# A table of offsets on the priorities of a list schedule

## The chip, the core and the metric

The kernel runs on one core of a Trainium2 chip. The core has engines that run side by side, each with its own queue of instructions: TensorE (PE in the profile, its weight loads PEld), VectorE (DVE), ScalarE (ACT), GpSimd (POOL), and SyncE (SP), which here only issues DMAs. The metric is the device time of one execution in microseconds; of several runs the median counts. TensorE's clock has two levels, 2.4 and 1.2 GHz; the profile's granted clock is 1.00 when a whole stretch was at the higher one.

## What is computed

The reference runs two networks one after the other on x (512 tokens, width 1024), in float32:

```python
# first_block
for i in range(2):
    h = rmsnorm(x, norm_mix[i])
    y = conformer_conv_module(h, ...) if i == 0 else nsa_attention(h, ...)
    x = x + y
    x = x + swiglu_ffn(rmsnorm(x, norm_ffn[i]), ...)
# second_block
for layer in range(2):
    mix = mamba2_mixer(h, ...) if layer == 0 else stick_breaking_attention(h, ...)
    h = layer_norm(ALPHA * h + mix, ...)
    h = layer_norm(ALPHA * h + squared_relu_mlp(h, ...), ...)
```

So there are eight phases, named conv, ffn0, nsa, ffn1, mamba, mlp0, sb and mlp1 in the kernel. The attention of nsa has 16 heads in 4 groups, rotary positions on a part of each head, compressed blocks and causal softmax.

## The kernel before

x lies in SBUF as eight tiles x_1 to x_8 of 128 features by 512 tokens, and every phase works on all 512 tokens. Each float32 product is made of three matmuls with operands split in a high and a low part (mm3: xh with whi at L135, xl with whi at L136, xh with wlo at L137); a product of one 128-column block of a weight with all of x is 8 x 3 = 24 matmuls of 128x512. Weights come by DMA from SyncE (wraw, L106), ACT rounds the high part (whi, L95) and DVE or POOL subtracts (wlo, L96), or, in other phases, ACT and an adding DMA make wlo (L121 to L123). Activations are split in the same way (L95/L96, L210/L211).

In the phase conv the queue of SyncE brings the first weight of the input projection, the tap weights of the depthwise convolution (conv_taps; their split parts are wh and wl) and the tiles of x.

In nsa each group of heads has a projection of k and four heads' worth of q. The rotation, turn (L773), copies parts of the rows by four small DMAs into sw, multiplies sw by the sines (L781, POOL) and x by the cosines (L782, POOL) and adds both (L783, DVE). For k the result tk is then spread by DMA and split (kdh, kdl); for q it is split into qa and qb (L1535 to L1538). scores (L986) makes the score block of a head in three PSUM banks (L997 to L1002), takes the negative maximum of each of its four parts (nmx, L1005, DVE), then the exponentials (pr, L1008, ACT); the banks are free after these. The probabilities are scaled (L1014, L1016), transposed (L1027), split (pth, ptl) and multiplied with v (L1041). compress makes a product with 160 columns for the compressed blocks, and L1057 the scores against these.

Layer norms of the second network are computed for two halves of the tokens (class HalfNorm; L312 and L314 add up sums, L329 adds squares, L162 and L152 to L156 make the scale rr by a Newton iteration, L183 turns it by TensorE), the second half beside the first matmuls of what follows.

What sets the order: the kernel's functions record all instructions of the program, each with a priority (the place in the program less an offset by a name, PRIO, given by pri). Then class Arrange (L1741) takes all instructions of the program, builds their dependences, prices each one, and runs a list schedule over all engines: schedule keeps one list of instructions for each engine, sorted by priority, and takes from it the first that could start at once, else the one that could start first; for SyncE it is always the first whose buffer is free. It models buffers, the DMA queue, the port shared by DVE and POOL, ACT's function tables and TensorE's two speeds. Its result, the order of each engine's instructions and of the takers of each buffer, is what apply (L1993) fixes. On the chip each engine runs its instructions in that order, and each waits for what it depends on.

Of the kernel before, what the change touches and what calls it, by code (L numbers as in the profile page):

```python
# [2134 lines left out]
```

## Time and profile before

| | |
|---|---|
| runs | 2943.2, 2943.57, 2951.58 us; median 2943.57 |
| profiled execution | 2945.75 us, of which span 2944.0 us, mean granted clock 0.97 |
| busy: TensorE, VectorE, ScalarE, GpSimd | 2792.5, 1710.5, 1488.9, 457.3 us |
| conv, ffn0 | to 250, to 600 us |
| nsa, ffn1 | 600 to 1050, to 1390 us |
| mamba, mlp0 | 1390 to 1900, to 2250 us |
| sb, mlp1 | 2250 to 2600, to 2944 us |

The times of the phases are rounded from the timeline. TensorE is the engine that is busy nearly all the time; how it stands in a stretch is read from the windows (busy time against length, and the granted clock), and what it waited for from the waits, where "A <- B" means that A was released by B. In timelines the bracket at the end of a row is the idle time of the engine ahead of it and what ended it.

### The profile page before, as it was taken

The page shows a single profiled execution, that of the slowest core. Times are in us where ns is not written, and L with a number is a line of the kernel's source. Part 1 is how long each engine was busy: PE and PEld are TensorE (multiplying, and loading weights), DVE is VectorE, ACT ScalarE, POOL GpSimd, SP SyncE. Part 2 cuts the span into 40 slices and gives each one's busy share as a digit, 9 for nine tenths or more (in the row PEclk, how much of TensorE's full clock was granted, in tenths as well). Part 3 has the DMA queues.
Part 4 walks back from the last instruction along what each step waited for, and adds up shares of the span by engine and source line. Part 5 has one row for each costly group of instructions (what it writes and reads, how often), then busy time and mean ns, then how long its engine had stood idle before and what let it go on. Part 6 is the DMA issues. An engine that isn't in the chain of part 4 may idle for free.

```text
span 2944.0 us, 38136 instructions
## 1 busy us (share of the span) xinstructions
PE 2792.5 (95%) x14613; PEld 2388.8 (81%) x14613; DVE 1710.5 (58%) x2946; ACT 1488.9 (51%) x2319; POOL 457.3 (16%) x440
## 2 busy tenths in 40 slices
PE   8989999999898899999999999799999999799997
PEld 7878888878777788887787878788888888788887
DVE  8976344546877944444775756743326566743335
ACT  4354222336566632223886877443334888543333
POOL 0010000034222100001111212400015222500004
PEclk9989999998999999999999999799999999899998
DMA  5323323221111133333556565333333544433232
GB/s 190 122 82 123 100 90 103 88 71 53 47 43 48 44 94 94 94 102 104 129 135 151 132 156 126 111 108 98 96 95 113 122 115 94 136 94 98 95 95 92
DMA packets 94919, 300.33 MB, mean 102 GB/s; under 512 B 11280, under 2 KB 13840, under 8 KB 94736
## 3 DMA queue, kind: packets, MB, share of 16 engines
q1 hardware_dynamic: 80192, 253.71, 27.6%
q0 software_dynamic: 14544, 44.18, 7.9%
q8 instruction: 115, 1.88, 0.3%
q14 instruction: 68, 0.56, 0.1%
HBM read 246.33 MB, written 2.10 MB: 84 GB/s over the span
## 4 chain that ended last, share of the span: by engine, by line
PE 57%; ACT 4%; DVE 3%; DMA 2%; issue 2%; POOL 0%; SPq 0%; ACTq 0%; POOLq 0%; DVEq 0%
PE mm L137 17%; PE mm L135 17%; PE mm L136 17%; DMA wlo<-wraw 2%; PE z L1670 1%; PE mm L1686 1%; DVE s L329 1%; PE e L1434 0%; ACT th L95 0%; ACT whi L121 0%; DVE x L538 0%; PE mm L1041 0%; PE st L183 0%; ACT s L1436 0%; ACT wlo L122 0%
## 5 line engine op out<-in xcount | busy, mean ns | idle before, releaser
L95 ACT ACTIVATE whi<-wraw 128x1024 fp32r<-128x1024 f32 (+2 forms) x383 | 385.1, 1009 | 1000.1 <-PE mm L136 769.0
L135 PE MATMUL mm<-xh,whi 128*128 128x512 f32 (+1 forms) x2240 | 849.2, 383 | 25.1 <-ACT whi L95 12.5
L137 PE MATMUL mm<-xh,wlo 128*128 128x512 f32 (+1 forms) x2240 | 851.2, 382 | 5.0 <-DMA wlo<-wraw 3.0
L136 PE MATMUL mm<-xl,whi 128*128 128x512 f32 (+1 forms) x2240 | 850.1, 381 | 0.9 <-DVE xl L543 0.6
L135 PEld LDWEIGHTS mm<-xh,whi 128*128 128x128 f32 x2240 | 425.9, 192 | 106.7 <-ACT whi L95 15.3
L137 PEld LDWEIGHTS mm<-xh,wlo 128*128 128x128 f32 x2240 | 427.5, 191 | 88.0 <-DMA wlo<-wraw 5.9
L136 PEld LDWEIGHTS mm<-xl,whi 128*128 128x128 f32 x2240 | 427.5, 191 | 78.2 <-DVE xl L543 1.7
L135 PE MATMUL mm<-hh,whi 128*128 128x512 f32 (+1 forms) x1344 | 483.3, 361 | 5.9 <-ACT whi L95 3.2
L137 PE MATMUL mm<-hh,wlo 128*128 128x512 f32 (+1 forms) x1344 | 483.2, 360 | 5.7 <-DMA wlo<-wraw 4.7
L136 PE MATMUL mm<-hl,whi 128*128 128x512 f32 (+1 forms) x1344 | 482.7, 360 | 0.9 <-DVE hl L96 0.9
L96 POOL TENSOR_TENSOR wlo<-wraw,whi 128x1024 fp32r<-128x1024 f32 (+2 forms) x119 | 255.1, 2155 | 1364.2 <-ACT whi L95 1342.5
L96 DVE TENSOR_TENSOR wlo<-wraw,whi 128x1024 fp32r<-128x1024 f32 (+1 forms) x264 | 316.3, 1200 | 183.6 <-ACT whi L95 180.8
L137 PEld LDWEIGHTS mm<-hh,wlo 128*128 128x128 f32 x1344 | 256.0, 191 | 44.1 <-DMA wlo<-wraw 6.0
L135 PEld LDWEIGHTS mm<-hh,whi 128*128 128x128 f32 x1344 | 256.0, 191 | 43.7 <-ACT hh L95 3.8
L136 PEld LDWEIGHTS mm<-hl,whi 128*128 128x128 f32 x1344 | 256.0, 191 | 36.9 <-DVE hl L96 1.4
L287 DVE TENSOR_TENSOR x<-x,mm 128x512 f32<-128x512 f32 x80 | 55.0, 687 | 222.3 <-PE mm L137 222.3
L123 POOL DMA_DIRECT2D wlo<-wraw x101 | 87.6, 867 | 485.8 <-ACT wlo L122 344.2
L96 DVE TENSOR_TENSOR hl<-s,hh 128x512 fp32r<-128x512 f32 (+1 forms) x120 | 88.2, 736 | 77.2 <-ACT hh L95 77.1
L121 ACT ACTIVATE whi<-wraw 128x1024 fp32r<-128x1024 f32 (+2 forms) x101 | 92.1, 912 | 75.8 <-PE mm L136 57.9
L503 DVE TENSOR_TENSOR s<-mm,rstd 128x512 f32<-128x512 f32 x44 | 30.4, 691 | 136.0 <-PE mm L137 136.0
L95 ACT ACTIVATE hh<-s 128x512 fp32r<-128x512 f32 (+1 forms) x120 | 75.7, 632 | 41.5 <-DVE s L504 27.3
L122 ACT ACTIVATE wlo<-wraw 128x1024 fp32r<-128x1024 f32 (+2 forms) x101 | 91.6, 908 | 8.0 <-PE mm L136 7.6
(459 smaller groups left out, 4072.1 us busy)
## 6 DMA issues: line engine op xcount, KB each, us to landing
wraw<-mlp_w SPq DMA_DIRECT2D x144, 512.0 KB
wraw<-ffn_w_in SPq DMA_DIRECT2D x88, 512.0 KB
wlo<-wraw POOLq DMA_DIRECT2D x68, 512.0 KB, 4.8
wraw<-ssm_w_in SPq DMA_DIRECT2D x48, 512.0 KB
wraw<-ffn_w_out SPq DMA_DIRECT2D x32, 448.0 KB
wraw<-conv_taps SPq DMA_DIRECT2D x20, 512.0 KB
wraw<-ssm_w_out SPq DMA_DIRECT2D x40, 256.0 KB
wraw<-conv_w_out SPq DMA_DIRECT2D x16, 512.0 KB
```

Of the source, the lines that this page charges most:

```text
L95: nc.scalar.activation(hi, x, AF.Copy)
L96: (eng or nc.vector).tensor_tensor(lo, x, hi.bitcast(F32), op=OP.subtract)
L121: self.nc.scalar.activation(hi[:, :n], raw[:, :n], AF.Copy)
L122: self.nc.scalar.activation(lo[:, :n], raw[:, :n], AF.Copy, scale=-1.0)
L123: self.nc.gpsimd.dma_start(lo[:, :n], raw[:, :n], accum_op=OP.add)
L135: mm(ps, ah, bh, start=start, stop=False)
L136: mm(ps, ah, bl, start=False, stop=False)
L137: mm(ps, al, bh, start=False, stop=stop)
L287: nc.vector.tensor_tensor(c.x[m], c.x[m], ps, op=OP.add)
L329: nc.vector.tensor_tensor(acc[m % 2], acc[m % 2], q, op=OP.add)
L503: nc.vector.tensor_tensor(u, pu, r, op=OP.mult)
L1670: nc.tensor.matmul(reg, w, part[:, ZOFF[jj]:ZOFF[jj] + S - jj * P], start=False, stop=True, skip_group_check=True)
```

## The change

A table DUE holds, for the phases conv, nsa, mamba and sb, an offset for each of 166 groups of instructions, from -2020 to +2520. A group is the engine, the name of the tile written and of the first two tiles read, without numbers ("DVE mx_nsp s_scr"; "D" for a tensor in DRAM). marks remembers where each phase begins in the list of instructions, and Arrange adds the group's offset of the phase to the priority of each instruction; a lower number is taken earlier. Nothing else is changed: the same instructions with the same operands and buffer sizes are scheduled, in another order. The closing norm of a phase, and the first weights of the phase behind it, belong to the phase. The search over the schedule's own estimate that the numbers are from is no part of the kernel.

```diff
@@ class Ctx @@
-        self.edges = []
+        self.edges, self.marks = [], []
...
+DUE = {
+    "conv": {
+        "DVE s_scr s_scr s_scr": -20, "DVE x2_xres x2_xres mm_pmm": -520, "DVE x4_xres x4_xres mm_pmm": -160, "DVE xl6_acts x6_xres par_const": 160,
...
+    "nsa": {
+        "ACT acc_acts hr_nq": -175, "ACT hh1_hid os_nsp": 80, "ACT pr_ntp mm_ps nmx_nsp": -705, "ACT pr_ntp pr_ntp sums_nsp": 5, "ACT pth_npp mm_ps": 5,
...
-    def __init__(self, tc, edges=()):
+    def __init__(self, tc, edges=(), marks=()):
...
         self.cost = [self.price(j) for j in range(n)]
+        self.due = [i.bass_priority or 0 for i in self.ins]
+        for (p, lo), hi in zip(marks, [m for _, m in marks[1:]] + [n]):
+            for j in range(lo, hi):
+                self.due[j] += DUE.get(p, {}).get(self.group(j), 0)
...
+    def group(self, j):
+        name = lambda a: self.tile(a).tag.rstrip("_0123456789") if self.tile(a) is not None else "D"
+        ins, outs = [[name(a) for a in x if hasattr(a, "ap")] for x in (self.ins[j].ins, self.ins[j].outs)]
+        return " ".join([("PE", "ACT", "DVE", "POOL", "SP", "", "")[self.eng[j]], (outs or ["-"])[0]] + ins[:2])
...
-        order, takers = self.schedule([i.bass_priority or 0 for i in self.ins])
+        order, takers = self.schedule(self.due)
...
             c.ph = p
+            c.marks.append((p, sum(len(b.instructions) for b in tc.nc.cur_f.blocks if b.name == tc.start_bb_name)))
...
-    Arrange(tc, c.edges).apply()
+    Arrange(tc, c.edges, c.marks).apply()
```

The order of SyncE's queue at the start. Rows are line, operation, tile written <- tensor read. Before:

```order
L106 DMA wraw_320<-conv_w_in 128x1024
L106 DMA wraw_403<-conv_taps 128x1024
L106 DMA wraw_409<-conv_taps 128x1024
L237 DMA par<-par 128x8
L242 DMA x_1_85<-x 128x512
L246 DMA wraw_93<-conv_w_in 128x512
L246 DMA wraw_94<-conv_w_in 128x512
L242 DMA x_2_86<-x 128x512
L242 DMA x_3_87<-x 128x512
L242 DMA x_4_88<-x 128x512
L246 DMA wraw_93<-conv_w_in 128x512
```

and now:

```order
L106 DMA wraw_320<-conv_w_in 128x1024
L237 DMA par<-par 128x8
L242 DMA x_1_85<-x 128x512
L246 DMA wraw_93<-conv_w_in 128x512
L246 DMA wraw_94<-conv_w_in 128x512
L242 DMA x_2_86<-x 128x512
L242 DMA x_3_87<-x 128x512
L242 DMA x_4_88<-x 128x512
L246 DMA wraw_93<-conv_w_in 128x512
L246 DMA wraw_94<-conv_w_in 128x512
L242 DMA x_5_89<-x 128x512
```

The two taps wraw_403 and wraw_409 go from ahead of x_1 to behind x_8 (six rows below the last one shown).

ACT in nsa, around the exponentials of one head (pr_7053; the tiles mm_7056, mm_7058 and mm_7057 are its scores, kdh the split of the next k, whi of later weights). Before:

```order
L1008 ACTIVATE pr_7053,sums_7055<-mm_7056,nmx_7054 128x128
L1008 ACTIVATE pr_7053,sums_7055<-mm_7056,nmx_7054 128x384
L95 ACTIVATE whi_7266<-wraw_7264 128x1024
L95 ACTIVATE whi_7533<-wraw_7531 128x1024
L95 ACTIVATE kdh_1242_7006<-s_7003 128x512
L95 ACTIVATE kdh_1245_7013<-s_7010 128x512
L1008 ACTIVATE pr_7053,sums_7055<-mm_7058,nmx_7054 128x512
L1008 ACTIVATE pr_7053,sums_7055<-mm_7057,nmx_7054 128x256
```

and now:

```order
L1008 ACTIVATE pr_7053,sums_7055<-mm_7056,nmx_7054 128x128
L1008 ACTIVATE pr_7053,sums_7055<-mm_7056,nmx_7054 128x384
L1008 ACTIVATE pr_7053,sums_7055<-mm_7058,nmx_7054 128x512
L1008 ACTIVATE pr_7053,sums_7055<-mm_7057,nmx_7054 128x256
L95 ACTIVATE hh_1247_7017<-os_6713 128x512
L95 ACTIVATE whi_7266<-wraw_7264 128x1024
L95 ACTIVATE pth_7154<-mm_7149 128x512
L1014 ACTIVATE pr_7053<-pr_7053,sums_7055 128x384
L95 ACTIVATE kdh_1242_7006<-s_7003 128x512
```

The four exponentials now stand in a row, ahead of the splits; a second head further on (pr_8010) has the same two orders.

DVE at the same place, the maxima of that head (nmx_7054) and the rotation of k (tk, L783). Before:

```order
L1016 TENSOR_SCALAR pr_6955<-pr_6955,sums_6957 128x128
L1016 TENSOR_SCALAR pr_6955<-pr_6955,sums_6957 128x256
L783 TENSOR_TENSOR tk_6605<-s_6993,s_6999 128x512
L96 TENSOR_TENSOR ptl_7050<-mm_7046,pth_7049 128x256
L96 TENSOR_TENSOR hl_1249_7019<-os_6713,hh_1247_7017 128x512
L1005 TENSOR_REDUCE nmx_7054<-mm_7058 128x1
L1005 TENSOR_REDUCE nmx_7054<-mm_7057 128x1
```

and now:

```order
L96 TENSOR_TENSOR ptl_7043<-mm_7037,pth_7042 128x512
L1005 TENSOR_REDUCE nmx_7054<-mm_7056 128x1 x2
L96 TENSOR_TENSOR ptl_7050<-mm_7046,pth_7049 128x256
L1005 TENSOR_REDUCE nmx_7054<-mm_7058 128x1
L1005 TENSOR_REDUCE nmx_7054<-mm_7057 128x1
L783 TENSOR_TENSOR tk_6605<-s_6993,s_6999 128x512
```

The rotation's sum went from ahead of the last two maxima to behind them.

POOL, two turns in nsa (s_6180 and s_6186, then s_6211 and s_6217). Before:

```order
L781 TENSOR_TENSOR s_6186<-sw_2483,sin_2446 128x512
L782 TENSOR_TENSOR s_6180<-s_6180,cos_2447 128x512
L96 TENSOR_TENSOR wlo_6577<-wraw_6574,whi_6576 128x1024
L1076 MEMSET pcz_6314 128x4x64
L781 TENSOR_TENSOR s_6217<-sw_2483,sin_2446 128x512
L782 TENSOR_TENSOR s_6211<-s_6211,cos_2447 128x512
```

and now:

```order
L782 TENSOR_TENSOR s_6180<-s_6180,cos_2447 128x512
L781 TENSOR_TENSOR s_6186<-sw_2483,sin_2446 128x512
L1076 MEMSET pcz_6314 128x4x64
L782 TENSOR_TENSOR s_6211<-s_6211,cos_2447 128x512
L781 TENSOR_TENSOR s_6217<-sw_2483,sin_2446 128x512
```

The product with the cosines (L782) comes ahead of that with sw (L781), here and in all 17 turns.

On TensorE the rows are the same with others between them: eight projections of 24 matmuls that stood in one piece in nsa stand in pieces of about 8 with scores, transposes and values between them, and the compress product stands among the pieces of a projection.

## Rows read from the trace of the kernel before

**Rows 1.** The page: busy time of each engine, and the chain that ended last.

```profile
PE 2792.5 (95%) x14613; PEld 2388.8 (81%) x14613; DVE 1710.5 (58%) x2946; ACT 1488.9 (51%) x2319; POOL 457.3 (16%) x440
...
PE 57%; ACT 4%; DVE 3%; DMA 2%; issue 2%; POOL 0%; SPq 0%; ACTq 0%; POOLq 0%; DVEq 0%
```

**Rows 2.** Windows: us, engines' busy time (count), granted clock, DMA share, GB/s.

```profile
250.00:600.00 350.00, 349.04 (x1525) 285.99 (x1524) 159.33 (x194) 102.69 (x128) 4.01 (x6) 1.00 0.29 92
...
sum 450.00, PE 403.46 PEld 344.16 DVE 328.59 ACT 260.98 POOL 121.53; mean PE 44.83 PEld 38.24 DVE 36.51 ACT 29.00 POOL 13.50
...
705.00:726.00 21.00, 17.40 (x90) 17.07 (x90) 8.26 (x27) 8.98 (x19) 7.30 (x4) 0.59 0.20 61
...
924.00:943.00 19.00, 14.99 (x65) 12.15 (x66) 13.37 (x36) 11.22 (x28) 2.62 (x2) 0.82 0.15 52
...
6.00:10.00 4.00, 0.00 (x0) 0.00 (x0) 3.31 (x4) 3.31 (x5) 0.00 (x0) 1.00 1.03 383
```

**Rows 3.** TensorE's waits, 600 to 1050: total us, times, longest.

```profile
PE mm L997 <- DVE qa L1537: 8.3, 2, 8.1
...
PE mm L997 <- ACT pr L1008: 5.7, 3, 2.7
...
PE mm L135 <- ACT v L95: 3.6, 1, 3.6
...
PE mm L1027 <- DVE tk L771: 2.9, 2, 1.6
...
PE mm L1041 <- DVE ptl L96: 2.8, 3, 1.2
```

**Rows 4.** Timeline from 0 to 14: start us, us, engine, line, operation.

```profile
7.75 1.06 ACT L95 ACTIVATE wh<-wraw 128x1024 fp32r<-128x1024 f32 x1 [0.28 <-DMA wraw<-conv_taps]
...
8.71 0.71 ACT L210 ACTIVATE xh<-x,par 128x512 fp32r<-128x512 f32 x1
...
10.51 0.80 PE L135 MATMUL mm<-xh,whi 128*128 128x512 f32 x1 [10.51 <-ACT whi L95]
```

**Rows 5.** Timeline from 820 to 847: rows of PE, DVE and ACT.

```profile
824.42 0.23 PE L1002 MATMUL mm<-cmask,identr 128*128 128x128 f32 x1
...
836.72 0.45 PE L997 MATMUL mm<-kdh,qb 128*128 128x128 f32 x1 [2.61 <-ACT pr L1008]
...
828.22 2.87 DVE L783 TENSOR_TENSOR tk<-s,s 128x512 f32<-128x512 f32 x1 [2.46 <-POOL s L782]
...
831.94 1.01 DVE L1005 TENSOR_REDUCE nmx<-mm 128x1 f32<-128x512 f32 x2
...
841.25 0.69 DVE L783 TENSOR_TENSOR t<-s,s 128x512 f32<-128x512 f32 x1 [1.17 <-POOL s L782]
...
834.14 0.63 ACT L95 ACTIVATE kdh<-s 128x512 fp32r<-128x512 f32 x1 [1.97 <-DMA s<-tk]
...
835.91 0.67 ACT L1008 ACTIVATE pr<-mm,nmx 128x512 f32<-128x512 f32 x1
```

**Rows 6.** Timeline from 752 to 768: rows of POOL, DVE and PE.

```profile
759.37 1.28 POOL L781 TENSOR_TENSOR s<-sw,sin 128x512 f32<-128x512 f32 x1 [1.36 <-DMA sw<-s]
...
760.59 1.28 POOL L782 TENSOR_TENSOR s<-s,cos 128x512 f32<-128x512 f32 x1
...
762.08 2.82 DVE L783 TENSOR_TENSOR t<-s,s 128x512 f32<-128x512 f32 x1
...
766.44 0.48 PE L997 MATMUL mm<-kdh,qa 128*128 128x128 f32 x1 [8.05 <-DVE qa L1537]
```

**Rows 7.** TensorE's waits, 1390 to 1900.

```profile
PE mm L137 <- DMA wlo<-wraw: 7.7, 9, 2.2
```

**Rows 8.** Timeline from 1873 to 1892: rows of DVE and POOL.

```profile
1877.86 5.45 DVE L329 TENSOR_TENSOR s<-s,s 128x256 f32<-128x256 f32 x3 [3.46 <-ACT s L328]
...
1873.28 12.23 POOL L96 TENSOR_TENSOR wlo<-wraw,whi 128x1024 fp32r<-128x1024 f32 x5 [0.49 <-ACT whi L95]
```

**Rows 9.** TensorE's waits, 2250 to 2600.

```profile
PE st L183 <- DVE rr L156: 8.5, 2, 4.5
```

More of the change, by code (lines that the diff above doesn't have):

```diff
@@ L1738, in sb_phase @@
         closing(c, "sb_w_o", [a[4:] + b for a, b in zip(hs, late[0])], 1, "lnmix1", head)
+DUE = {
+    "conv": {
+        "ACT hh7_hid y7_convy": 120, "ACT s_scr y1_convy": 585, "DVE hl5_hid y5_convy hh5_hid": -80, "DVE rsq_small rsq_small rv_small": 410,
+        "DVE s_scr s_scr s_scr": -20, "DVE x2_xres x2_xres mm_pmm": -520, "DVE x4_xres x4_xres mm_pmm": -160, "DVE xl6_acts x6_xres par_const": 160,
+        "DVE y3_convy st_pst y3_convy": 960, "DVE y3_convy y3_convy st_pst": 320, "PE mm_pmm hh5_hid whi_wts": 20, "PE mm_pmm hh5_hid wlo_wts": 630,
+        "PE mm_pmm hl1_hid whi_wts": 640, "PE mm_pmm hl7_hid whi_wts": 290, "PE mm_pmm ul_convu wh_convt": 110, "PE mm_pmm xh1_acts whi_wts": 310,
+        "PE st_pst ones_const acc_acts": -640, "SP wraw_convr D": 160, "SP x5_xres D": 20, "SP x6_xres D": 140, "SP x7_xres D": -950
+    },
+    "nsa": {
+        "ACT acc_acts hr_nq": -175, "ACT hh1_hid os_nsp": 80, "ACT pr_ntp mm_ps nmx_nsp": -705, "ACT pr_ntp pr_ntp sums_nsp": 5, "ACT pth_npp mm_ps": 5,
+        "ACT qb_nq t_nq": -320, "ACT s_scr hl0_hid": 1080, "ACT s_scr t_nq": -140, "DVE hl0_hid hd_nk hh0_hid": 1555, "DVE hl0_hid s_scr s_scr": 1165,
+        "DVE hr_nq hv_nq": 160, "DVE hr_nq rsq_small hr_nq": -325, "DVE kdl1_nkv s_scr kdh1_nkv": 585, "DVE kvl_nk hh1_hid v1_nk": 365,
+        "DVE kvl_nk hl0_hid v1_nk": 895, "DVE mx_nsp s_scr": -1110, "DVE nmx_nsp mm_ps": -10, "DVE os_nsp mm_ps os_nsp": 10,
+        "DVE pr_ntp pr_ntp sums_nsp": -55, "DVE qa_nq t_nq qa_nq": -640, "DVE qb_nq t_nq qb_nq": 40, "DVE s_scr hh0_hid par_const": -540,
+        "DVE s_scr hh1_hid par_const": -320, "DVE s_scr hl0_hid par_const": -15, "DVE s_scr t_nq qg8_nconst": 365, "DVE sums_nsp sums_nsp": -40,
+        "DVE t_nq mm_ps rstd_hid": -90, "DVE t_nq s_scr s_scr": -950, "DVE v1_nk mm_ps v1_nk": -605, "DVE vcl_nk mm_ps vch_nk": -80,
+        "DVE vt0h_nconst vch_nk": 960, "DVE vt0l_nconst vcl_nk": 70, "DVE vt1h_nconst vch_nk": -285, "DVE x0_xres x0_xres mm_ps": -420,
+        "DVE x1_xres x1_xres mm_ps": -420, "DVE x2_xres x2_xres mm_ps": -40, "PE mm_ps cmask_nconst identr_nconst": -290,
+        "PE mm_ps hh1_hid whi_wts": -520, "PE mm_ps hl0_hid whi_wts": 10, "PE mm_ps hl1_hid whi_wts": 5, "PE mm_ps ident_const acc_acts": -250,
+        "PE mm_ps ident_const pcz_nk": -240, "PE mm_ps ident_const tk_nk": 5, "PE mm_ps kdl0_nkv qa_nq": 25, "PE mm_ps pth_npp v1_nk": -30,
+        "PE mm_ps ptl_npp v0_nk": -150, "PE mm_ps w2h_nk hh0_hid": 455, "PE mm_ps xh2_acts wlo_wts": 265, "PE mm_ps xh6_acts wlo_wts": -1130,
+        "PE mm_ps xh7_acts whi_wts": -185, "PE mm_ps xh7_acts wlo_wts": -105, "PE mm_ps xl3_acts whi_wts": 35, "PE mm_ps xl5_acts whi_wts": 1020,
+        "POOL s_scr sw_nconst sin_nconst": 40, "POOL wlo_wts wraw_wts whi_wts": 95, "SP wraw_wts D": -20
+    },
+    "mamba": {
+        "ACT bth_mb e_pe": 320, "ACT cb_mb e_pe": -490, "ACT cy_mb mm_pmm par_const": -10, "ACT hh3_hid yt_mb par_const": 880, "ACT s_scr e_pe": -30,
+        "ACT whi_wts wraw_wts": 20, "ACT wlo_wts wraw_wts": 50, "ACT xd0_mk s_scr": -640, "ACT xwh_mb s_scr": -150, "DVE cy_mb u40_mk par_const": 20,
+        "DVE cy_mb u41_mk par_const": -30, "DVE i2f_mk ident_const ident_const": -480, "DVE prl_mb s_scr prh_mb": 780,
+        "DVE rsq_small rsq_small rv_small": 160, "DVE s_scr s_scr cb_mb": 650, "DVE s_scr s_scr s_scr": 30, "DVE x3_xres x3_xres mm_pmm": -40,
+        "DVE x4_xres st_pst x4_xres": -80, "DVE x4_xres x4_xres par_const": 250, "DVE x5_xres st_pst x5_xres": 155, "DVE x5_xres x5_xres mm_pmm": 135,
+        "DVE x6_xres x6_xres mm_pmm": -530, "DVE x7_xres x7_xres mm_pmm": 95, "DVE xl3_acts x3_xres xh3_acts": 325, "DVE xl6_acts yt_mb par_const": 640,
+        "DVE xl7_acts yt_mb par_const": 360, "DVE yt_mb yt_mb e_pe": -1110, "PE e_pe ch_mb bh_mb": -5, "PE e_pe ch_mb bl_mb": -50,
+        "PE e_pe cl_mb bh_mb": -25, "PE e_pe cl_mb prh_mb": 10, "PE e_pe ident_const rr_small": 10, "PE e_pe mh0_mb xd1_mk": 5,
[4 rows of a table added]
+    },
+    "sb": {
+        "ACT kb_skv mm_pmm": -695, "ACT qb_skv mm_pmm": 50, "ACT qh_skv qa_skv": 15, "ACT qh_skv qb_skv": 640, "ACT s_scr mm_pmm": -10,
+        "ACT t_st z_pz": -20, "ACT th_st t_st": 90, "ACT wlo_wts wraw_wts": -5, "ACT x1_xres x1_xres par_const": -530,
+        "ACT x4_xres x4_xres par_const": 1745, "ACT xh2_acts x2_xres par_const": 475, "ACT xh5_acts x5_xres par_const": -640,
+        "ACT xh6_acts x6_xres par_const": 770, "DVE ka_skv mm_pmm ka_skv": -320, "DVE kb_skv mm_pmm kb_skv": -215, "DVE s_scr s_scr s_scr": -1645,
+        "DVE t_st z_pz": -80, "DVE x1_xres st_pst x1_xres": 1055, "DVE x2_xres st_pst x2_xres": 250, "DVE x3_xres st_pst x3_xres": 960,
[4 rows of a table added]
+        "PE mm_pmm xl0_acts whi_wts": 155, "PE z_pz qh_skv kb_skv": -1170, "PE z_pz th_st none_sk": 5, "POOL wlo_wts wraw_wts": -440,
+        "SP qb_skv qb_skv": 2520, "SP wraw_wts D": 855
+    },
+}
```

8 rows, old and new, of the table DUE are left out of this document.

## The prediction

> **What bounds the kernel now.** I read the page's busy shares first: TensorE works 2792.5 us of a span of 2944.0 [rows 1], so all its waiting is 151.5 us, and nothing else is there to be won by an order, except time in which it works at its lower clock. The chain of waits says the same: matmuls are by far its largest share [rows 1]. Next the windows, to see where the waiting lies. In the dense stretch from 250 to 600 us TensorE is busy 349.04 of 350 at a granted clock of 1.00 [rows 2]; the two MLPs and the second FFN look alike. The table has no entries for those phases and nothing could come of one. The nine windows of the attention stage "nsa" hold 403.46 of 450 busy, so 46.5 us of waiting [rows 2], and the clock falls there: 0.59 from 705 to 726, 0.82 from 924 to 943 [rows 2]. Of its two levels, 2.4 and 1.2 GHz, a mean g over a stretch T means a share (1-g)/0.5 at the lower one; work done there takes twice its time. For 705 to 726 that is 0.82 x 21 = 17.2 us at 1.2 GHz, of which 3.6 us are the wait ahead of the compress product, so at most (17.2-3.6)/2 = 6.8 us are lost by the clock; for 924 to 943 0.36 x 19 = 6.8 us, at most 3.4 lost. Last the waits of TensorE in "nsa" by cause, then the timelines around the largest.
>
> The change adds and removes no instruction, so no busy time of its own: every term below is a wait that gets shorter or longer, or the clock beside it. It is made against the profiled execution, 2945.75 us, which lies 2.18 above the median of the runs (2943.57).
>
> **1. The start.** The queue of SyncE brings two tap weights (0.5 MB each) ahead of the first activation x_1, and ACT splits them (wh, 1.06 us each) ahead of x_1's split: wh at 7.75, then xh at 8.71, then the weight's split, and TensorE starts at 10.51 [rows 4]. Afterwards both stand behind x_8. 1.05 MB at the 383 GB/s of this stretch [rows 2] are 2.7 us; ACT has no other work there. So TensorE starts about 2.8 us sooner. The taps now land behind all of x, but the first matmul that uses them stands behind the whole first projection, which is the cover; with that gone the price is that of the load itself, 2.7 us back. I take 2.5, bounds 0 and 5 (the upper end if x_6 to x_8, ahead of which up to 2 MB less stand, also bring what follows forward).
>
> **2. Two heads whose softmax stood behind other work.** At 824.42 the score block of one head is done; the next score block (L997) needs its PSUM banks, which the exponentials (L1008) free. DVE takes the maxima of the last two parts (L1005) only at 831.94, since L783 stands ahead of them in its order: it waits for POOL, starts at 828.22 and takes 2.87 us [rows 5]. ACT's exponential then stands behind two weight splits and two kdh splits, the first at 834.14 waiting for a DMA, and starts at 835.91; TensorE goes on at 836.72 after 2.61 us of waiting [rows 5]. The same pattern comes once more, around 925. By cause the three kinds of waits in it are 5.7, 2.9 and 2.8 us in eight pieces, 11.4 in all [rows 3]; 10.8 of that lies in these two places. In the new order only one row of 0.4 us stands between these maxima, L783 behind them, and no split between the exponentials: DVE can have them by 827, ACT by 829. At the same time the projection that stood whole in front of the next block is cut in three: 24 matmuls were 5.5 us, 8 are 1.8, so the work that covers the chain goes from 9.5 us (824.6 to 834.1, where the wait begins) to about 6.7 (5.5 less, 1.8 and four matmuls of 0.23 more), that is to 831.3. 829 is before 831.3: the wait goes, and the other two thirds cover the transposes behind it. What is late next is the kdh split, needed for the following group only. Gain 10.8 if all goes; the clock behind the second wait gives up to 3.4 (above), behind the first about as much. I take 9 + 2 = 11, bounds 0 (new waits of that size) and 16.
>
> **3. The 8 us wait for the first query of a group.** L997 waits 8.05 us at 766.44 for DVE's qa [rows 6]. The chain to it is two rotations (turn, L773), of k and of q: each has L781 on POOL (1.28, waits for the swap DMAs), then L782 (1.28), then L783 on DVE (2.82) [rows 6]. L782 needs no DMA; it now stands ahead of L781 in all 17 turns, where POOL is idle, which takes 1.3 us from the chain per turn, 2.6 in two. qa's last step moves ahead of three small rows of DVE, 0.9. On the other side 1.8 us of work that stood ahead of the chain's start now stands behind it (nine matmuls of the compress output and seven of L1057, some 0.1 each). 8.05 - 2.6 - 0.9 - 1.8 = 2.7 remain; 5.3 gained, and of the half clock that follows 1.2. I take 6.5, bounds 0 and 10.
>
> L783's 2.82 or 2.87 against 0.69 at 841.25 [rows 5, 6] stand beside weight subtractions on POOL. The Trainium skill, "SBUF — State Buffer", section "Who interferes with whom", says that a DVE instruction with two SBUF inputs and a POOL instruction that reads SBUF exclude each other and that the later one waits for the whole of the other; these rows agree with it. By that rule the swap of L781 and L782 leaves L783 as long as it was, which is how I count it.
>
> **4. The compress product.** The 3.6 us wait [rows 3] is for v, at the end of a rotation. Of the projection that ran ahead of it whole, eight matmuls (1.8 us) now stand behind the first third of the compress matmuls, and the rotation is 1.3 shorter. I take 1.5 of the wait and 2.5 of the at most 6.8 of the clock: 4, bounds 0 and 10.4.
>
> **5. The rest of "nsa".** 46.5 - 10.8 - 8.05 - 3.6 = 24 us in many smaller waits. Other projections are cut in thirds too, which helps some and takes cover from others. I take 2, bounds -8 and 14.
>
> **6. "mamba".** Nine waits for split weights that come by DMA are 7.7 us [rows 7]; the order puts the whi products of two banks ahead of the first wlo product, which gives a few matmuls of cover (0.227 us each, 24 in 5.5 us) at each. I take 3, bounds 0 and 7.7. In its closing norm three L329 on DVE take 5.45 us beside five POOL subtractions of 2.4 (12.23 in all) [rows 8]; now L312 and two L314, of the same kind of operands, stand among them, and the chain for the scale behind them is no longer mixed with other rows. By the skill's rule above each one moved there costs up to a POOL instruction, 2.4 us. From the rows: in 12.23 us POOL lets some five such DVE rows through in either order, and what was behind the chain is done ahead of it: 0, bounds -5 and 2.
>
> **7. "sb".** Its closing has the same chain, half of the 8.5 us of L183 in this stretch [rows 9], and DVE no longer mixes it with other rows: 2. At its start the qb copies on SyncE's queue go behind weight loads; that queue issues in order, so a copy can wait behind a load whose buffer is not free. Bounds -6 and 5.
>
> Sum: 2.5 + 11 + 6.5 + 4 + 2 + 3 + 0 + 2 = 31. 2945.75 - 31 = 2914.75; I say 2914 as some of the 2.18 above the median is noise. The bounds taken all at once are +19 and -70; they won't come together.
>
> **Rivals.**
> A. The waits come back (within 8.8 us, 0.3%, which is about what a measurement of this kernel can tell from no change). The covers of 1.8 us are thin, the same work must fill all holes, and an order that fits one chain takes cover from another. For it: 24 us of "nsa" are already scattered waits. Against it: terms 1 to 3 shorten chains, not only covers. If terms 2 to 5 give a quarter (23.5 / 4 = 6) and the others nothing but the start (2.5), 2945.75 - 8.5 = 2937; if less, up to 2946.
> B. Slower: the thirds leave the softmax chain uncovered. Eight attention projections that were whole are cut; each loses 2.8 us of cover ahead of the next score block. If maxima and exponentials still come as late as 12.3 us after the scores (824.42 to 836.72) [rows 5], as when DVE stays held up by L783 or POOL, each of the eight waits 2.8 longer: 22 us, and TensorE at half clock behind it, some 1.5 us each, 12. Against this stand terms 1 and 3 to 7, 20: 2945.75 + 34 - 20 = 2960. It turns slower than before where the chain exceeds the new cover of 6.7 us by 2 or more at all eight. Against: the order of DVE and ACT takes out just these two obstacles.
> C. All holes filled: 2 to 5 at their upper bounds with the start: 5 + 16 + 10 + 10.4 + 14 + 7.7 = 63, 2883.
> D. The order isn't carried out as the table sets it: then the same time, 2944. The order of each engine's rows does differ, so I give it nothing beyond A.
>
> **How the numbers follow.** My forecast, a gain between 12 and 52, gets 0.70; A 0.15; C 0.05; B 0.10. The range leaves out C below and B and the worst of A above: 2892 to 2943. Faster by over 0.3% takes the forecast, C and a little of A: 0.78. Same 0.13, slower 0.09.
>
> **What would show it.** TensorE's first matmul near 7.7 us; at the two heads no wait over 1 us of L997 on the exponentials; the wait on qa under 4; TensorE's idle in "nsa" near 25 instead of 46.5 and no stretch of 20 us at 0.59; the busy time of TensorE lower by the clock alone, 5 to 10 us. Wrong would be: waits of L997 after many heads (B), SyncE's queue ahead of weights in "sb", or DVE rows of 2.4 us in a row in the closing norms.

## The result and the profile after

The changed kernel takes 2924.05 us (median of four runs, 2922.21 to 2925.07) against 2943.39 in the runs beside it, a ratio of 0.9933 with a 95% interval of 0.9913 to 0.9953: 19.3 us faster. The forecast was 2914, its range 2892 to 2943. The profiled execution is 2923.68 us, its span 2922.0. On the page after, the busy times (as in [rows 1]):

```profile
PE 2779.8 (95%) x14613; PEld 2377.2 (81%) x14613; DVE 1719.3 (59%) x2946; ACT 1486.0 (51%) x2317; POOL 461.0 (16%) x440
```

TensorE is busy 12.7 us less and idle 142.2 us instead of 151.5. So more than half of the gain isn't shorter waiting. Most of that part is work at the higher clock: by the granted clock of the two traces TensorE was at 1.2 GHz for 152.4 us instead of 175.3, which is worth up to half the difference, 11.5 us.

To see where, the two traces are cut at the same four matmuls, in the middle of the four dense MLP stretches, where the order of both kernels is the same: the ones that start at 400.00, 1200.16, 2050.21 and 2750.20 before. They start at 395.81, 1190.60, 2030.26 and 2727.74 after. The pieces are named by the phase inside: conv, nsa, mamba, sb, and the end. Windows of the first four before (stretch, length, busy times with counts of PE, PEld, DVE, ACT, POOL, then granted clock, DMA share, GB/s):

```profile
0.00:400.00 400.00, 373.20 (x2026) 321.80 (x2027) 282.37 (x461) 161.33 (x233) 23.49 (x25) 0.98 0.37 121
400.00:1200.16 800.16, 752.66 (x3731) 631.56 (x3730) 489.98 (x973) 365.61 (x714) 125.53 (x81) 0.96 0.23 70
1200.16:2050.21 850.05, 818.65 (x4141) 689.95 (x4139) 494.84 (x886) 499.31 (x743) 123.78 (x120) 0.98 0.47 121
2050.21:2750.20 699.99, 670.20 (x3751) 590.44 (x3750) 361.53 (x487) 385.52 (x514) 145.39 (x198) 0.97 0.38 106
```

and after:

```profile
0.00:395.81 395.81, 374.44 (x2026) 323.21 (x2027) 279.65 (x461) 162.63 (x233) 23.93 (x25) 0.98 0.37 123
395.81:1190.60 794.79, 746.33 (x3732) 623.61 (x3730) 490.37 (x973) 365.78 (x714) 126.39 (x81) 0.97 0.23 71
1190.60:2030.26 839.66, 813.21 (x4141) 687.57 (x4140) 506.55 (x886) 496.88 (x741) 124.80 (x120) 0.98 0.47 123
2030.26:2727.74 697.48, 668.04 (x3751) 587.74 (x3750) 361.01 (x487) 383.58 (x514) 146.79 (x198) 0.97 0.37 107
```

Length less PE's busy time is the idle time. The time at 1.2 GHz is worked out as in the prediction, from the granted clock before it is rounded to two places.

| piece | forecast, us | measured | idle before, after | at 1.2 GHz before, after |
|---|---|---|---|---|
| conv | -2.5 | -4.2 | 26.8, 21.4 | 17.1, 17.1 |
| nsa | -23.5 | -5.4 | 47.5, 48.5 | 64.9, 51.2 |
| mamba | -3 | -10.4 | 31.4, 26.4 | 37.5, 30.7 |
| sb | -2 | -2.5 | 29.8, 29.4 | 41.0, 37.5 |
| end | 0 | +0.4 | 16.1, 16.5 | 14.9, 15.8 |
| sum | -31 | -22.1 | | |

Sign and size are near the forecast, but the sum hides two misses of opposite sign. In nsa the waiting did not fall at all. TensorE's waits there after the change (answering to [rows 3]):

```profile
PE mm L997 <- DVE qa L1537: 9.5, 2, 6.7
PE mm L691 <- ACT acc L688: 7.9, 4, 4.4
PE mm L1041 <- DVE ptl L96: 7.2, 8, 2.6
PE mm L135 <- ACT hh L95: 4.7, 2, 3.9
...
PE mm L997 <- DVE s L812: 2.6, 2, 1.4
...
PE mm L997 <- ACT pr L1008: 0.7, 2, 0.5
```

The wait on the exponentials fell from 5.7 to 0.7 us, that on v (3.6) is gone, and that on qa is 6.7 where 8.05 stood and 2.7 was forecast. In their place stand waits on L688's acc (7.9, of 2.8 before), on ptl (7.2, of 2.8), on hh behind the compress product (4.7) and on L812's s (2.6).

### The profile page after: what moved, and what is told of

Read it like the earlier page. It is cut to its first block, busy times and chain, and to the rows that moved or that the text cites. A ratio compares the mean times of both kernels' runs of the same rounds, so it can differ in the third digit from the quotient of the medians.

```text
span 2922.0 us, 38131 instructions
## 1 busy us (share of the span) xinstructions
PE 2779.8 (95%) x14613; PEld 2377.2 (81%) x14613; DVE 1719.3 (59%) x2946; ACT 1486.0 (51%) x2317; POOL 461.0 (16%) x440
## 4 chain that ended last, share of the span: by engine, by line
PE 57%; DVE 3%; ACT 3%; issue 2%; DMA 2%; SPq 0%; ACTq 0%; POOL 0%; POOLq 0%
PE mm L135 17%; PE mm L137 17%; PE mm L136 17%; DMA wlo<-wraw 1%; PE z L1670 1%; PE e L1434 1%; DVE s L329 1%; DVE acc L314 0%; PE mm L1686 0%; ACT th L95 0%; PE e L136 0%; PE e L137 0%; ACT t L1652 0%; ACT wlo L122 0%; DVE x L538 0%
## 5 line engine op out<-in xcount | busy, mean ns | idle before, releaser
L135 PE MATMUL mm<-xh,whi 128*128 128x512 f32 (+1 forms) x2240 | 846.5, 382 | 22.3 <-ACT whi L95 9.9
L135 PEld LDWEIGHTS mm<-xh,whi 128*128 128x128 f32 x2240 | 424.8, 191 | 101.0 <-ACT whi L95 12.2
L135 PE MATMUL mm<-hh,whi 128*128 128x512 f32 (+1 forms) x1344 | 478.9, 360 | 6.6 <-ACT whi L95 3.6
L135 PEld LDWEIGHTS mm<-hh,whi 128*128 128x128 f32 x1344 | 254.6, 190 | 45.3 <-issue 3.5
```

The source lines that it names most:

```text
L135: mm(ps, ah, bh, start=start, stop=False)
```

## The experiments

All kernels differ from the changed one in the table, in one function, or in both. The ratio of each is that of its mean to the mean of the kernel before, run beside it on the same chip (whose medians there were 2945.75, 2944.76 and 2944.96). Lengths of pieces, idle times and waits are those of the one profiled execution.

### One phase's entries at a time

```diff
-DUE = { "conv": ..., "nsa": ..., "mamba": ..., "sb": ... }
+DUE = { "nsa": ... }
```

The other three keep one phase's entries in the same way.

> The whole table of nsa, none for conv, mamba and sb. If each phase's entries act in their own phase: 794 to 796 us between the two points as in the changed kernel, all other stretches as before the change (400.0, 850.0, 700.0), and the whole 5 us faster than before. Rival: the gain of nsa hangs on what conv leaves behind: 800, no difference.

> The table of mamba alone. If the 10.4 us that the stretch from the middle of ffn1 to the middle of mlp0 became shorter (850.0 to 839.7) come from its own entries: 838 to 841 there. Rival (half of it is the clock, which falls at other moments when the stretch begins at another moment, also in an unchanged order: the kernel with nsa's table alone had 844.4 there): 843 to 847. The other stretches as before the change, within 2 us.

> The table of conv alone. If the start is what conv gains: TensorE's first matmul at 7.7 us as after the change (10.5 before), and 395 to 397.5 us to the middle of ffn0 (400.0 before, 395.8 after). If the gain needs nothing else, nsa 800 and mamba 850 stay within 3 us; the whole 2938 to 2942.

> The table of sb alone. If its entries make the 2.5 us of the stretch from the middle of mlp0 to the middle of mlp1 (700.0 before, 697.5 after the change): 696 to 698 there, the whole 2940 to 2943. Rival (the clock alone): 699 to 700.

| table of | median, ratio and interval | its own piece | the other pieces against before |
|---|---|---|---|
| nsa | 2930.40, 0.9949 [0.9934, 0.9963] | 800.2 to 792.3 | conv +1.0, mamba -5.6, sb -0.6 |
| mamba | 2933.47, 0.9964 [0.9952, 0.9977] | 850.0 to 837.3 | conv +1.4, nsa +3.0, sb -1.3 |
| conv | 2944.29, 1.0000 [0.9991, 1.0010] | 400.0 to 394.8 | nsa +4.2, mamba -2.9, sb -0.7 |
| sb | 2942.78, 0.9994 [0.9985, 1.0004] | 700.0 to 695.6 | conv +2.2, nsa 0.0, mamba -3.6 |

Each phase's entries act in their own piece, as expected; the four pieces came out 0.2 to 1.7 us below the ranges given for them. But the pieces without entries don't stay as they were, nsa's table gives 15 us as a whole where 5 were forecast, and the table of conv, with 5.2 us less in its own piece, gives nothing as a whole where 2938 to 2942 us were forecast. What happens there is seen in the piece nsa of three kernels whose order there is that of before: with the tables of mamba and sb the rows of TensorE, DVE, ACT and POOL stand in the same order, and with that of conv two matmuls and at most 30 of DVE's 973 rows stand elsewhere. The windows with the tables of mamba, sb and conv:

```profile
401.40:1204.57 803.17, 756.59 (x3732) 635.77 (x3730) 490.12 (x973) 365.39 (x714) 125.44 (x81) 0.95 0.23 70
...
402.24:1202.38 800.14, 753.49 (x3732) 632.42 (x3730) 489.90 (x973) 365.88 (x714) 125.38 (x81) 0.96 0.24 70
...
394.82:1199.13 804.31, 758.07 (x3732) 636.12 (x3730) 493.39 (x973) 365.71 (x714) 125.66 (x81) 0.95 0.23 70
```

Idle is 46.6, 46.6 and 46.2 us, as before (47.5). The busy time is 756.6, 753.5 and 758.1 of the same matmuls (752.7 before), and the time at 1.2 GHz 75.1, 68.3 and 78.5 us (64.9 before). So beside the same waits TensorE's clock costs more or less from one trace to the next, by up to 4 us of this piece's length. In mamba the eight kernels of this study that lack its entries lie at 844.4 to 847.8, mean 846.2, while the profiled execution of the kernel before has 850.0; the five that have them lie at 836.3 to 839.7, mean 837.9. So its entries are worth some 8 us, and the other 2 of the -10.4 in the table of the pieces belong to the two executions compared there. In the same way nsa's entries are worth about 8 (792.3 to 795.2 in three kernels against 800.1 to 804.3 in four), conv's about 6 (mean 395.6 of five against 401.5 of nine), sb's about 2 (696.7 of five against 699.0 of nine). These add up to 24 us where the whole gained 19.3, and conv's 6 were not seen in the whole when its entries stood alone, so each is good to a few us only.

### The softmax rows and the cut of the projections

Two kernels take up one of the two parts on which term 2 rests, a third both. In all three conv, mamba and sb have no entries. The first line is nsa_soft, the second nsa_thirds; nsa_softthirds has the four entries of both. The two entries of nsa_thirds stand in the changed kernel's table with these values. Of nsa_soft only that of the exponentials does: the table takes the maxima earlier by 10, nsa_soft by 700. So nsa_soft shows what a stronger push of the softmax rows does, and not what the table's own entries do alone.

```diff
-DUE = { "conv": ..., "nsa": ..., "mamba": ..., "sb": ... }
+DUE = {"nsa": {"ACT pr_ntp mm_ps nmx_nsp": -705, "DVE nmx_nsp mm_ps": -700}}
...
+DUE = {"nsa": {"PE mm_ps xh2_acts wlo_wts": 265, "PE mm_ps xl5_acts whi_wts": 1020}}
```

> The table holds two groups of nsa alone: the exponentials (L1008, -705) and the maxima (L1005, -700) are taken earlier; the projections stay whole. Theory S (the softmax rows of DVE and ACT made the two waits at 836 and 925): the waits of L997 on the exponentials fall from 5.7 us to under 1, and the time from the middle of ffn0 to the middle of ffn1 (800.2 us before, 794.8 after the change) to 793 to 796. Rival T (the cut of the projections in thirds does it): no gain, 799 to 801, the waits come back at the transposes and values (L1027, L1041).

> The table holds two groups of nsa alone, which cut the projections in thirds (xh2 with wlo +265, xl5 with whi +1020); DVE's and ACT's order at the two heads stays as before the change. Theory S: 799 to 803 us between the same two points, as the chain behind a head's scores is as long as before and has less cover. Rival T: 794 to 797.

> Both pairs of groups of nsa together. Theory S with the thirds as filler: 790 to 795 us, the lowest of the three. If the thirds cost cover: 796 to 799, worse than the softmax pair alone.

| kernel | median, ratio and interval | nsa | idle, us | at 1.2 GHz, us |
|---|---|---|---|---|
| nsa_soft | 2963.22, 1.0047 [1.0028, 1.0065] | 820.4 | 53.8 | 99.0 |
| nsa_thirds | 2959.29, 1.0048 [1.0030, 1.0066] | 810.6 | 51.4 | 81.9 |
| nsa_softthirds | 2976.49, 1.0102 [1.0081, 1.0122] | 827.2 | 60.8 | 99.0 |
| only_nsa (all 56 entries) | 2930.40, 0.9949 [0.9934, 0.9963] | 792.3 | 41.2 | 58.0 |

The windows of the piece nsa of nsa_soft and of only_nsa:

```profile
403.20:1223.56 820.36, 766.52 (x3732) 643.33 (x3730) 488.31 (x973) 366.99 (x714) 124.77 (x81) 0.94 0.23 69
...
400.98:1193.27 792.29, 751.10 (x3731) 628.91 (x3730) 490.64 (x973) 364.83 (x714) 127.87 (x81) 0.96 0.24 71
```

Every forecast of the length for these three was wrong, by both theories. By the ratios each part makes the kernel 14 us slower, and both together cost 30. In the traces most of it is not waiting: of the 20.2 us that nsa is longer in nsa_soft, 6.3 are idle time and 13.9 are TensorE's own busy time, with 34 us more at 1.2 GHz. The runs of one kernel lie far apart here (2947.7 to 2965.6 for nsa_soft, 2950.1 to 2970.4 for nsa_thirds, where those of the kernel before beside them lie within 8.6 us), and the profiled execution of nsa_soft is the highest of its seven, so its piece is long for its mean; that of nsa_thirds is the second lowest of seven and that of nsa_softthirds the lowest of four, so theirs are short. What nsa_soft shows is where the wait went (its waits in nsa, and rows of DVE, ACT and PE around 884):

```profile
PE mm L691 <- ACT acc L688: 17.5, 6, 4.8
...
881.44 0.16 DVE L156 SCALAR_TENSOR_TENSOR hr<-rsq,hr 128x8 f32<-128x8 f32 x1
...
883.56 0.62 ACT L688 ACTIVATE acc<-hr 128x512 f32<-128x512 f32 x1
...
884.23 1.11 PE L691 MATMUL mm<-ident,acc 128*128 128x128 f32 x4 [4.75 <-ACT acc L688]
```

No wait of L997 on the exponentials is left, so the mechanism of term 2 is right as far as it goes. But DVE's maxima and ACT's exponentials now stand ahead of the small rows that make the head norm's scale: the last of them (L156) ends at 881.6, L688 comes behind the rest of a head's exponentials and two of their scalings (L1014) at 883.56, and TensorE waits 4.75 us for it, 17.5 in all where it was 2.8.

### The rows that were pushed back, taken earlier too

```diff
 DUE = {"nsa": {"ACT pr_ntp mm_ps nmx_nsp": -705, "DVE nmx_nsp mm_ps": -700,
+    "ACT acc_acts hr_nq": -1000, "DVE hv_nq mm_ps": -1000, "DVE hr_nq hv_nq": -1000, "DVE rsq_small hr_nq hr_nq": -1000,
+    "DVE rsq_small rsq_small hv_nq": -1000, "DVE hr_nq rsq_small hr_nq": -1000}}
```

> The softmax pair of nsa (exponentials and maxima earlier) and, with it, the rows of the head norm's scale earlier by 1000 (L680, L152 to L156 on DVE, L688 on ACT). With the pair alone L691 waited 17.5 us for L688, in pieces of up to 4.8, since the small Newton rows and L688 stood behind maxima and exponentials. Theory S2 (the pair's gain was lost at that chain): the waits of L691 on L688 fall to under 6 us, those of L997 on the exponentials stay under 1.5, and nsa (820.4 us between the middles of ffn0 and ffn1 with the pair alone, 800.2 before the change) is 796 to 806. Rival K (the engines' time is short as a whole and any row taken earlier costs another): other waits take the place, 812 to 822.

2957.66 us, ratio 1.0042 [1.0027, 1.0057]; nsa 812.9, idle 50.5, 92.2 us at 1.2 GHz. The waits on L688 fell to 0.8, as theory S2 has it, and yet nsa is within the range of rival K: the wait on qa is 8.4 again (2.6 with the pair alone), and L1027 waits 11.4 on pr (8.3 with the pair alone, 2.4 before the change). Idle time is only some 3 us less than with the pair alone. Entries that cure one wait make others; of the two, K is what the runs support. Which of the 56 entries hold the balance in the full table was not tried one by one.

### The two products of the rotation

The changed kernel runs L782 (cosines) ahead of L781 (sines), and term 3 counted 2.6 us for it. The end of the chain after (SP, POOL, DVE, ACT and PE, answering to [rows 6]):

```profile
753.47 0.66 SPq L779 DMA_DIRECT2D sw<-s  x1
...
755.62 1.42 POOL L782 TENSOR_TENSOR s<-s,cos 128x512 f32<-128x512 f32 x1 [8.10 <-DMA sw<-s]
757.00 1.26 POOL L781 TENSOR_TENSOR s<-sw,sin 128x512 f32<-128x512 f32 x1
...
758.29 2.81 DVE L783 TENSOR_TENSOR t<-s,s 128x512 f32<-128x512 f32 x1 [2.41 <-POOL s L781]
...
761.14 0.63 ACT L1536 ACTIVATE qb<-t 64x512 fp32r<-64x512 f32 x1 [4.54 <-DVE t L783]
761.78 0.63 ACT L1535 ACTIVATE qa<-t 64x512 fp32r<-64x512 f32 x1
...
763.88 1.19 PE L997 MATMUL mm<-kdh,qa 128*128 128x128 f32 x3 [6.70 <-DVE qa L1537]
```

L782 starts only at 755.62, 2.15 us after the last of the four swap DMAs was issued, and the trace names that DMA as its releaser, as it named it for L781 before. L782 writes its product over x, and the DMAs still read x. The first in the line waits for them, whichever it is. This is the term of the prediction that was wrong outright: "L782 needs no DMA". Then qb's copy (761.14) goes ahead of qa's (761.78), another 0.6.

```diff
-            m2 = c.s()[:n]
-            nc.gpsimd.tensor_tensor(m2, m[:n], sn[:n], op=OP.mult)
-            nc.gpsimd.tensor_tensor(x, x, cs[:n], op=OP.mult)
-            nc.vector.tensor_tensor(out, x, m2, op=OP.add)
+            m2, m3 = c.s()[:n], c.t(k1, [P, S], F32, "xc")[:n]
+            nc.gpsimd.tensor_tensor(m3, x, cs[:n], op=OP.mult)
+            nc.gpsimd.tensor_tensor(m2, m[:n], sn[:n], op=OP.mult)
+            nc.vector.tensor_tensor(out, m3, m2, op=OP.add)
```

> The changed kernel, with the cosine product of turn written to a tile of its own (xc) instead of over x. Theory W (the swap of the two POOL products gave nothing, since the cosine product overwrites the x that the swap DMAs still read, and so waits for them as the sine product does): the cosine product now starts about 1 us after x is there, while the DMAs run, L783 1.3 us sooner in each rotation, and the wait of L997 on qa (6.70 us after the change) falls to 3.5 to 5; nsa (794.8 us between the middles of ffn0 and ffn1) by 1 to 4. Rival V (POOL was held by something else, or the chain is longer elsewhere): the wait stays 6 to 7.

2913.35 us, ratio 0.9890 [0.9866, 0.9915]. The same chain (line 781 is now the cosine product, 782 the sine product):

```profile
752.94 0.75 DVE L812 SCALAR_TENSOR_TENSOR s<-t,qg,mm 128x512 f32<-128x512 f32 x1
...
760.81 2.82 DVE L783 TENSOR_TENSOR t<-xc,s 128x512 f32<-128x512 f32 x1 [1.26 <-POOL s L782]
...
753.83 1.30 POOL L781 TENSOR_TENSOR xc<-s,cos 128x512 f32<-128x512 f32 x1 [0.29 <-DVE s L812]
759.47 1.30 POOL L782 TENSOR_TENSOR s<-sw,sin 128x512 f32<-128x512 f32 x1 [4.34 <-DMA sw<-s]
...
757.24 0.66 SPq L779 DMA_DIRECT2D sw<-s  x1
...
765.79 1.19 PE L997 MATMUL mm<-kdh,qa 128*128 128x128 f32 x3 [4.68 <-DVE qa L1537]
```

The cosine product starts 0.14 us after x is there, while the DMAs run. L783 follows the last DMA's issue by 3.57 us (757.24 to 760.81), where it was 4.82 (753.47 to 758.29): the 1.25 us of one POOL product that were forecast for the swap. The wait on qa is 4.68, in the range of theory W. nsa is 791.8 us, idle 40.4 instead of 48.5. The whole is 10.7 us below the changed kernel, and the tile accounts for a part at most: of the 7.4 us between the two profiled executions 3.0 lie in nsa and the rest in pieces that the edit doesn't touch, and in nsa the scheduler made another order (hundreds of rows of TensorE and DVE stand elsewhere).

> The kernel before the change, without the table, with the cosine product of turn in a tile of its own. Theory W: the rotation is 1.3 us shorter in each of its two turns, the wait of L997 on qa (8.05 us) falls to 5 to 6.5, nsa 800.2 to 795 to 800, the whole 1 to 6 us faster. Rival: what the tile of its own gave beside the table came from the new order that the scheduler made for it, and here it is within 1 us of before or slower.

The same edit without any table: 2941.88 us, ratio 0.9985 [0.9974, 0.9997].

```profile
PE mm L1041 <- DVE ptl L96: 11.9, 5, 4.8
...
PE mm L997 <- DVE qa L1537: 0.6, 1, 0.6
...
402.35:1203.23 800.88, 758.41 (x3731) 636.48 (x3730) 497.41 (x973) 366.21 (x714) 125.83 (x81) 0.95 0.23 70
```

The wait on qa is gone (0.6), L1041's on ptl is 11.9 where 2.8 stood, idle is down by 5.0 to 42.5, and the piece is 800.9 long, as before: TensorE's busy time is 5.8 us higher, with 78.5 us at 1.2 GHz where 64.9 stood. So the whole of what was won in waiting went to the clock in this execution. The runs give 3 us by the medians, 4.4 by the means (0.9 to 7.7), which is theory W's range and doesn't quite shut out the rival (within 1 us). But the wait and the piece miss W's ranges (5 to 6.5, 795 to 800), and the wait fell further than the tile can make it: in this order L783 of that chain stands beside no subtraction of POOL and takes 0.69 us instead of 2.82.

> The changed kernel without the one entry of nsa that takes qb's copy (L1536) earlier by 320, so that qa's copy (L1535) comes first again. If the order of the two costs at the start of a group: the wait of L997 on qa falls from 6.70 by 0.6, nsa is 793.5 to 795. Rival: neighbouring orders change too and the clock with them, 795 to 800.

```diff
-"ACT qb_nq t_nq": -320,      # nsa
```

2922.53 us, ratio 0.9928 [0.9911, 0.9945]; the longest wait on qa fell from 6.70 to 5.63, nsa is 795.2, in the rival's range, the whole not to be told from the changed kernel.

> The changed kernel with the cosine product in a tile of its own, and qa's copy ahead of qb's again. If the two gains at the start of a group add up: the wait of L997 on qa 4.1 (4.69 with the tile alone), the whole 2911 to 2914. If neighbouring orders and the clock decide, as with qa_first alone (2922.5 against 2924.1): 2908 to 2918, not to be told from the tile alone.

Both edits together: 2915.26 us, ratio 0.9903 [0.9879, 0.9926], two of its four runs at 2909 and two at 2921, in the range forecast for the case that neighbouring orders and the clock decide. Its wait on qa is down to 0.6 and its nsa to 782.7 in the profiled execution, the shortest of all, with 41.0 us at 1.2 GHz; over all runs it isn't told from turn_apart. The wait is shorter than the sum of the two edits makes it (4.1 was forecast): here too L783 stands beside no subtraction of POOL (0.68 us instead of 2.81). All runs of both kernels lie below those of the changed one (2922.2 to 2925.1), though the intervals of the ratios overlap a little.

## Why the prediction was right, and where it was not

**Term 1, the start,** was right: the rows answering to [rows 4] are

```profile
5.92 0.72 ACT L210 ACTIVATE xh<-x,par 128x512 fp32r<-128x512 f32 x1 [0.71 <-DMA x<-x]
...
7.73 0.80 PE L135 MATMUL mm<-xh,whi 128*128 128x512 f32 x1 [7.73 <-ACT whi L95]
```

2.78 us sooner, for 2.8 forecast. The other 1.4 us of conv (3 by the means of all kernels) come with waits in the taps that shrank too (wlo 1.5 to nothing, uh 1.4 to nothing, y 1.7 to 1.1). By the means conv is past the bound of 5 by 1.

**Term 2, the two heads:** the order did what was said. Rows of DVE, ACT, POOL and PE at the first of them, answering to [rows 5], and under them L1010 in the kernel before (least, median and most ns of its 32 places):

```profile
826.83 1.01 DVE L1005 TENSOR_REDUCE nmx<-mm 128x1 f32<-128x512 f32 x2
828.50 0.69 DVE L783 TENSOR_TENSOR tk<-s,s 128x512 f32<-128x512 f32 x1 [0.66 <-POOL s L781]
...
827.59 0.69 ACT L1008 ACTIVATE pr<-mm,nmx 128x512 f32<-128x512 f32 x1
...
830.97 2.36 DVE L1010 TENSOR_TENSOR sums<-sums,gat 128x4 f32<-128x4 f32 x1
833.25 0.73 DVE L812 SCALAR_TENSOR_TENSOR s<-t,qg,mm 128x512 f32<-128x512 f32 x1
...
845.96 1.76 DVE L1010 TENSOR_TENSOR sums<-sums,gat 128x4 f32<-128x4 f32 x1
847.64 0.68 DVE L96 TENSOR_TENSOR ptl<-mm,pth 128x512 fp32r<-128x512 f32 x1
...
830.37 2.93 POOL L96 TENSOR_TENSOR wlo<-wraw,whi 128x1024 fp32r<-128x1024 f32 x1 [1.91 <-ACT whi L95]
...
845.32 2.38 POOL L96 TENSOR_TENSOR wlo<-wraw,whi 128x1024 fp32r<-128x1024 f32 x1 [4.44 <-ACT whi L95]
...
834.13 0.36 PE L997 MATMUL mm<-kdh,qb 128*128 128x256 f32 x1 [1.20 <-DVE s L812]
...
848.38 0.44 PE L1041 MATMUL mm<-ptl,v 128*128 128x384 f32 x1 [1.77 <-DVE ptl L96]
...
L1010 DVE TENSOR_TENSOR sums<-sums,gat x32: 152/164/168, 658.2 to 998.1; 128x4 f32<-128x4 f32 x32
```

The last maxima are done at 827.8, the last exponentials before 829, L783 comes behind and is no longer stretched (0.69). But L997 still waits, 1.20 us for the bank that L812 reads, and L1041 1.77 for ptl; at the second head 1.37 and 2.63. 7.0 of 10.8 us are back under other names, so 4 were gained and not 9. The clock did better than counted: between 791 and 1011 us only 3.4 us are at the lower level, where there were 17 in the same part before. Other stretches lost some of it again: the one at 759 has 20.5 us at the lower level where 13.7 stood. The step that failed is "the other two thirds cover the transposes behind it". The rows show what stood in the chain instead: L1010, a multiplication of 128x4 numbers that took 0.15 to 0.17 us in all its 32 places before, takes 2.36 and 1.76 us here, to the end of a POOL subtraction that began before it, as L783 did before the change. L812 and ptl, on which L997 and L1041 wait, come directly behind it. At the second head it is the same (2.34 and 1.73 us beside POOL). So the obstacle moved from L783 to a smaller row. Without the 1.6 to 2.2 us of each, by an estimate from these rows, 5.7 of the 7.0 us would not be there; no run moved L1010 alone.

**Term 3, the wait on qa:** forecast 2.7 us left, 6.70 measured. 2.6 of the difference were counted for a swap that gives nothing; with a tile of its own for the product (turn_apart) 2.0 of the wait go. Another part is the copy of qb, 0.64 by the rows above, 1.07 of waiting in qa_first. The 0.9 of "qa's last step moves ahead of three small rows" didn't come either: from the end of L783 to the start of qa it is 1.95 us (761.10 to 763.05) where it was 0.80, since besides the copy of qb two other rows of DVE (L771, L1072) stand ahead of it. With both edits 0.6 is left of the wait; 2.1 us of what went there are L783, which is no longer stretched.

**Term 4, the compress product:** its wait of 3.6 is gone, and 3.94 us of waiting stand behind it at 733.45 (L135 on hh) and 5.99 ahead of it at 690 and 692 (L691 on acc, 4.42 and 1.57), where 0.78 stood. At the lower clock it is 17.0 us in two stretches (10.2 at 687, 6.8 at 732), where it was 17.1 in one. So the term is zero or below, at the lower end of its bounds. hh's split stands behind a head's four exponentials on ACT (730.74 to 732.87), and in the chain ahead of the first L691 the row L155, of 128x16 numbers, takes 2.04 us beside a POOL subtraction (0.16 without). These waits don't come from nsa's entries as such: with nsa's table alone (only_nsa) the waits on v, on hh and of L691 are 0.7, 1.2 and 2.4 us in all of nsa, and the piece is idle for 41.2. The same 56 entries gave another order when the scheduler came to nsa from another conv.

**Term 5, the rest of nsa,** can't be told from what came in place of terms 2 to 4. As a sum, nsa was forecast at -23.5 and came at -5.4 (about -8 by the mean of several kernels). The mis-sized part is the one that rival A described: "an order that fits one chain takes cover from another". A was given 0.15 for the whole kernel; for nsa alone it is what happened to the waits of this kernel. Rival B's effect was seen in nsa_thirds, where only the projections are cut: slower by 14 us, but not by the waits of L997 that B counted. Those on the exponentials fell to 0.7 us there, while the transposes (L1027) wait 11.7 us on pr (2.4 before) and L691 10.6 on L688.

**Term 6, mamba:** the waits for split weights fell from 7.7 [rows 7] to 4.9 us, 2.8 for 3 forecast. Waits of TensorE there after:

```profile
PE st L336 <- DVE s L329: 8.5, 1, 8.5
...
PE mm L137 <- DMA wlo<-wraw: 4.9, 6, 1.5
PE st L183 <- DVE rr L156: 2.7, 1, 2.7
```

In the closing norm TensorE waits 8.5 (L336 on L329) and 2.7 us (L183 on rr) where it was 5.1 and 5.3, 0.8 more in all, inside the bounds around the 0 that was forecast. At a norm inside the phase (tile e, L183 on rr) it is 5.5 for 4.3. DVE's rows beside POOL's, answering to [rows 8]:

```profile
1854.87 4.16 DVE L329 TENSOR_TENSOR s<-s,s 128x256 f32<-128x256 f32 x2
1858.95 2.56 DVE L314 TENSOR_TENSOR acc<-acc,x 128x256 f32<-128x256 f32 x1
...
1851.28 12.44 POOL L96 TENSOR_TENSOR wlo<-wraw,whi 128x1024 fp32r<-128x1024 f32 x5 [0.50 <-ACT whi L95]
```

Three of them take 6.7 us beside five POOL subtractions, about one POOL instruction each. This agrees with the rule of the Trainium skill ("SBUF — State Buffer", "Who interferes with whom") cited ahead. A price of 2.4 us for each moved row, which the prediction named and did not take, would have been too high here, since in both orders only three or four of them meet POOL. What was left out are waits of 1.2 to 1.6 us by line in the gates (L171, L1362, L1434), all gone, and the clock: the piece came at -10.4 for -3, some 8 of it from the entries by the comparison above. Of the 5.0 us of waiting that went, these and wlo are the most; the busy time fell by 5.4, and 6.8 us less at 1.2 GHz explain half their length of it, 3.4. The other 2 stay without a cause.

**Term 7, sb:** -2.5 for -2. Its piece is 695.6 to 697.9 with its entries and 696.9 to 700.0 without, so the 2 us hold for the means alone.

So the time came into the range, which was wide enough for it, although nsa fell short by 18 us; mamba and conv gave 9 more than was counted, and that these misses have opposite signs was luck. Of the signs that were named, TensorE's first matmul near 7.7 us and no wait over 1 us on the exponentials came true; the wait on qa under 4 (6.70), an idle time in nsa near 25 (48.5 in the piece) and no stretch of 20 us at the lower clock (20.5 from 759) did not. The forecast's sign rested on terms 1 to 3, the start and nsa; with one phase's entries alone the runs show a gain for nsa (15 us) and mamba (11), and none for conv, whose 6 us stand in its own piece alone.

## What to carry to other kernels

When a list schedule's order is changed, a wait that goes has to be followed to the next waiting instruction of the same engines: rows of DVE and ACT taken earlier push others back, and two of nsa's 56 entries, those that cut the projections, alone made this kernel slower by 14 us that together with the rest make it faster by 15. Above all look at which rows of DVE now stand beside the subtractions of POOL: a row of 128x4 numbers held up there for 2.36 us was as dear as the large one that was moved away. A swap of two instructions shortens a chain only if the one that goes first really needs less: an operation in place needs every reader of its old value, DMAs among them, and a tile of its own took off this chain the 1.25 us that the swap did not. Price such a change by stretches cut at the same matmul in both traces, with idle time and time at the lower clock apart, and take the same stretch from several kernels before a few us in it are put down to an edit.
